# Expert weights from expert 11 on: gate and up in 22 KB pieces through three slot pairs, down tiles in single slots

## The chip, the core and the metric

The kernel runs on one core of a Trainium2 chip. The metric is device time in microseconds (us), the median of the runs. The weights lie in HBM and are brought into the core's own memory (SBUF) by DMA while TensorE (PE in the rows) multiplies. All weight transfers are issued from the queue of SyncE (SP, and SPq for its queue), one after the other in the order in which they stand there; an issue that waits holds up all that stand behind it.

## The reference: what is computed

One block of an encoder on 512 tokens of width 1024: a Fourier mixer and a state-space mixer, merged by gates, then a channel mixer of 16 experts, then a gated per-layer input and a last norm. The stage of this case is the mixer of experts:

```python
def expert_choice_ffn(h, w_router, w_gate, w_up, w_down):
    cap = EC_CAPACITY * s // N_EXPERTS            # 2 * 512 // 16 = 64 rows
    affinity = jax.nn.softmax((h @ w_router).astype(jnp.float32), axis=-1)
    vals, idx = lax.top_k(jnp.swapaxes(affinity, 1, 2), cap)
    xg = h[bidx, idx]
    hid = jax.nn.silu(jnp.einsum('becd,edf->becf', xg, w_gate)) * jnp.einsum('becd,edf->becf', xg, w_up)
    y = jnp.einsum('becf,efd->becd', hid, w_down) * vals[..., None].astype(h.dtype)
    ...
```

Each of the 16 experts takes 64 tokens and has three float32 matrices: gate and up of 1024 x 2816, down of 2816 x 1024. That is 11.5 MB each, 34.6 MB for an expert, and each byte is used once.

## The kernel before, in words

The experts run one after the other (L1867 on). An expert's part on TensorE is first `gate_up` (L1478): eight row blocks k of gate and up, 128 rows each, are multiplied with the 64 chosen tokens, whose transposed rows are the stationary operand. A piece of 128 x 2816 (one row block, 11 KB in each partition) feeds 6 matmuls in the source, which the trace counts as 12. Then the hidden rows are formed in three units of 512, 512 and 384 columns (`UNITS`, L957; ScalarE and VectorE, then a transpose on TensorE, L1508), and `down` (L1512) multiplies each unit with its tiles of the down matrix.

Weights come through a ring of ten slots of 11 KB, which lie two by two in five pairs (`big`, L952; tiles `wp` in the rows; pair 0 is named wp_2840, pair 1 wp_3047, pair 2 wp_2406, pair 3 wp_2528, pair 4 wp_2647). Beside them there are short slots of 8 KB, made from buffers that earlier work has left (`small`; tiles `w`). `weight_stream` (L977) lists all pieces in the order of use. `prefetch` (L1003) gives the next piece a slot by `take` (L1030) and records its DMA (L1017); if there is no slot the list waits. `done` (L1066), called where the matmuls of a piece end, gives its slot back and calls `prefetch(2)`. So the program fixes which piece follows which in a slot, and its DMA waits for the matmuls of the slot's former piece.

`paired(e)` (L965) is true for experts 0 to 5. Their gate and up rows come two row blocks at a time, 22 KB in each partition, into a whole pair, and their down tiles have three or four blocks (12 or 16 KB), also in a pair. From expert 6 on each piece takes one slot: gate and up come as 16 pieces of 11 KB, and down as 11 tiles of two blocks (8 KB). By then some slots hold things for good: `fin` (half of pair 0), `sel` (half of pair 1), and the four tiles `pg` of the per-layer gate matrix, of which three lie in short slots and the fourth in half of pair 4. `take` gives a down tile a short slot if one is free (`own`, which holds once `pg` 3 has its place), and otherwise a slot of the ring. From expert 11 on this leaves pairs 2 and 3 whole, one half each of pairs 0, 1 and 4, and three short slots.

The order on TensorE is written out by hand (`with ordered(E.PE)`): between the steps of `gate_up` and `down`, `spend` (L1826) puts in other work from two lists, by costs that each step yields: ranking, gathering and transposing for the next expert (L1461, L1662, L1421), and from expert 7 on the finish of rows that an expert has changed (L1705, L1729, L1742, L1748). The order on the other engines, SP's among them, is set by a scheduler, which places an instruction by what it waits for. GpSimd (POOL) issues the indirect fetches and stores of token rows.

Of the kernel before, what the change touches and what calls it, by code (L numbers as in the profile page):

```python
# [25 lines left out]
NE = 16  # L26
REDO = 9
SLACK = 0.9
START = 0
NSEL = 4  # L30
WX = 2.0
OPEN = 3
# [81 lines left out]
def block_kernel(ctx, tc, ins, cst, out, n_exp=NE, dbg=None, upto="end"):  # L114
# [837 lines left out]
    big, small = list(range(10)), []  # L952
# [12 lines left out]
    def paired(e):  # L965

        return e < NB - 1

    def down_tiles(e, u):

        q = UNITS[u][2]
        if paired(e):
            return [[(h, a) for a in range(q)] for h in range(2)]
        return [[(h, a), (h, a + 1)] for h in range(2) for a in range(0, q - 1, 2)] + (
            [[(h, 2) for h in range(2)]] if q == 3 else [])

    def weight_stream():  # L977
        for e in range(n_exp):
            if e == EMB:
                yield ("p", 0), None  # L980
                yield ("pp", 0), rows(ins["w_ple_proj"], 0)
                for i in range(2):
                    yield ("E", i), None
            if e == NB - 1:
                yield ("fin", 0, 0), None
                yield ("sel", 0, 0), None
            if e == NB:
                for i in range(4):
                    yield ("pg", i), rows(ins["w_ple_gate"], 2 * i)
            n = 2 if paired(e) else 1  # L990
            for k in range(0, 8, n):
                for w, nm in ((wg_, "g"), (wu_, "u")):
                    yield (e, nm, k), dap(w, (e * D + k // 2 * 2 * P + k % 2) * FE, [[2 * FE, P], [1, n * FE]])
            for u, (f0, _, q) in enumerate(UNITS):
                for i, blocks in enumerate(down_tiles(e, u)):
                    (h, a), (h1, _) = blocks[:2]
                    yield (e, "d", u, i), dap(wd_, (e * FE + h * HALF + f0 + a) * D,
                                              [[q * D, P], [HALF * D if h1 != h else D, len(blocks)], [1, D]])
# [21 lines left out]


    halves_left = {0: {0, 1}, 1: {2, 3}}
    pair_tiles = {}

    def slot_view(i, n=1):
        if i // 2 not in pair_tiles:
# [3 lines left out]
    def take(key):  # L1030


        rows_ = key[0] != "E" and len(key) == 3
        own = isinstance(key[0], str) and key[0] != "m" or ("pg", 3) in wt
        uid[0] += 1
        if not isinstance(key[0], str) and paired(key[0]):
            i = next((i for i in big if i % 2 == 0 and i + 1 in big), None)
            if i is None:
                return None
            big.remove(i)  # L1040
            big.remove(i + 1)
            home[key] = i, 2
            t = slot_view(i, 2)
            if not rows_:
                q = UNITS[key[2]][2]
                t = t[:, :q * D].rearrange("p (a n) -> p a n", a=q)
            wt[key] = t
        elif own and small and not rows_:
            pool, tag = home[key] = small.pop(0)
            t = pool([P, 2, D], f"w{uid[0]}", F32R if tag == "hl" else F32, tag=tag, bufs=2 if tag == "hl" else 1)  # L1050
            wt[key] = t[:].bitcast(F32) if tag == "hl" else t[:]
        else:
            alone = [i for i in big if i ^ 1 not in big]
            if not big:
                return None
            i = alone[0] if alone and own else big[0]
            big.remove(i)
            home[key] = i, 1
            t = slot_view(i)
            wt[key] = t if rows_ else t[:, :2 * D].rearrange("p (a n) -> p a n", a=2)  # L1060
        return wt[key]
# [100 lines left out]
    rows_, logs = {}, {}  # L1162
# [314 lines left out]

    def gate_up(e):  # L1478
        pgu = {nm: [xbank("g", 6) for _ in UNITS] for nm in "gu"}
        m = 2 if paired(e) else 1  # L1480
        for k, nm, j in [(k, nm, j) for k in range(0, 8, m) for nm in "gu" for j in range(m)]:
            w = get_w((e, nm, k))
            for pp, (f0, n, _) in zip(pgu[nm], UNITS):
                for h in range(2):
                    c0 = j * FE + h * HALF + f0
                    T.matmul(pp[64 * h:64 * h + 64, :n], XGT[e][:, (k + j) % 4, (k + j) // 4], w[:, c0:c0 + n],  # L1486
                             start=k + j == 0, stop=k + j == 7)
            if j == m - 1:
                done((e, nm, k))
            if k + j < 7 or nm == "g":  # L1490
                yield 1.0
        for u, (pg, pu, (_, n, _)) in enumerate(zip(pgu["g"], pgu["u"], UNITS)):
            t = ht
            S.activation(t[:, :n], pg[:, :n], AF.Tanh, scale=0.5)  # L1494
            V.scalar_tensor_tensor(t[:, :n], t[:, :n], 1.0, pg[:, :n], OP.add, OP.mult)  # L1495
            V.scalar_tensor_tensor(hids[u % 2][:, :n], t[:, :n], 0.5, pu[:, :n], OP.mult, OP.mult)  # L1496
            if u == 0:
                yield 1.0
            turn_hidden(e, u)
            yield 0  # L1500
# [432 lines left out]
```

## Time and profile before

| | us |
|---|---|
| median of 3 runs | 1737.38 |
| the three runs | 1737.38, 1733.82, 1737.91 |
| the profiled execution | 1737.61 |
| its span, first to last instruction | 1735.6 |
| around the span | 2.0 |

The span has three stretches: the mixers up to about 370 us, the experts up to about 1715 us, and 20 us of last rows. In the views a window is given in us from the start of the span; the DMA share is the mean busy share of the 16 DMA engines, and GB/s is what they moved. A row of the timeline has the start, the duration, the engine and line, the operation with its tiles, and in brackets how long the engine stood idle before it and who ended that. A row of a chain has a start, a duration and what took it; for a DMA the duration runs from its issue to its landing. Granted clock 1.00 is 2.4 GHz, 0.5 is 1.2 GHz. A row `PE ... <- DMA ...: a, n, b` says that PE waited a us in n waits for that transfer, the longest b.

### The profile page before, as it was taken

To read this page: it belongs to the slowest core of one execution; us is meant where nothing else is said; L and a number is where in the kernel's file an instruction comes from. 1 tells how busy PE (TensorE), PEld (TensorE's weight loads), DVE (VectorE), ACT (ScalarE), POOL (GpSimd) and SP (SyncE) were. 2 spreads that over 40 slices of the span, in tenths; PEclk is the share of its full clock that TensorE was granted. 3 is DMA by queue.
4 is the path that set the end of the run, shared out by engine and by line. 5 is a ranking of instruction groups with operands and counts; after the bars stand their busy time and mean duration, and the time that the engine had idled before them with its cause. 6 is when DMAs were issued, how large, how long until landed. Compare 5 with 4: busy or idle time off the path is not lost.

```text
span 1735.6 us, 19348 instructions
## 1 busy us (share of the span) xinstructions
PE 1584.8 (91%) x7982; PEld 746.5 (43%) x7982; DVE 509.1 (29%) x1063; ACT 350.2 (20%) x649; POOL 86.2 (5%) x134
## 2 busy tenths in 40 slices
PE   7998979999979998989886899999999998999896
PEld 6776768743323333323222344434344343433332
DVE  6898857332212021211111221212211112112011
ACT  4367443232101111010101010111111111111000
POOL 1000000110000000000000100000101000000000
PEclk9999989999999999999998999999999999999999
DMA  7622819589999999999999999999999999999994
GB/s 161 134 67 68 135 50 277 198 302 407 430 427 428 399 428 430 427 428 428 407 420 420 422 400 421 371 421 422 421 421 421 422 420 406 420 421 421 421 423 184
DMA packets 116440, 613.07 MB, mean 353 GB/s; under 512 B 25880, under 2 KB 59184, under 8 KB 72320
## 3 DMA queue, kind: packets, MB, share of 16 engines
q1 hardware_dynamic: 111648, 597.27, 87.3%
q0 software_dynamic: 4544, 14.49, 2.2%
q8 instruction: 63, 1.03, 0.3%
q14 instruction: 25, 0.20, 0.0%
q10 hardware_dynamic: 160, 0.07, 0.0%
HBM read 599.54 MB, written 12.78 MB: 353 GB/s over the span
## 4 chain that ended last, share of the span: by engine, by line
PE 42%; DMA 34%; ACT 1%; DVE 1%; issue 1%; SPq 0%; POOL 0%; POOLq 0%; ACTq 0%; DVEq 0%
PE px L1486 18%; DMA wp<-in_w_exp_gate_dram 14%; DMA wp<-in_w_exp_up_dram 13%; PE px L1521 12%; DMA wp<-in_w_exp_down_dram 5%; PE px L1748 3%; DMA w<-in_w_exp_down_dram 3%; PE px L1643 3%; PE px L1508 1%; PE px L1612 1%; PE px L1396 1%; PE px L1705 1%; ACT hT L1510 0%; PE px L1784 0%; PE px L1421 0%
## 5 line engine op out<-in xcount | busy, mean ns | idle before, releaser
L1486 PE MATMUL px<-wp,xgT 128*64 128x512 f32 (+1 forms) x3072 | 645.9, 566 | 65.8 <-DMA wp<-in_w_exp_gate_dram 47.7
L1486 PEld LDWEIGHTS px<-wp,xgT 128*64 128x64 f32 x3072 | 211.4, 138 | 473.1 <-issue 368.8
L1521 PE MATMUL px<-wp,hT 128*64 128x512 f32 x1200 | 281.4, 608 | 23.0 <-DMA wp<-in_w_exp_down_dram 15.8
L1521 PEld LDWEIGHTS px<-wp,hT 128*64 128x64 f32 x1200 | 81.0, 138 | 183.8 <-issue 142.8
L1242 DVE SCALAR_TENSOR_TENSOR junk<-xraw,aff,before 128x512 bf16<-128x512 f32 x60 | 44.9, 749 | 181.9 <-ACT xraw L1462 181.4
L1495 DVE SCALAR_TENSOR_TENSOR xraw<-xraw,px 128x512 f32<-128x512 f32 (+1 forms) x48 | 30.9, 643 | 129.0 <-ACT xraw L1494 128.8
L179 DVE TENSOR_TENSOR hl<-raw,hl 128x1024 fp32r<-128x1024 f32 (+1 forms) x45 | 53.8, 1198 | 38.4 <-ACT hl L178 38.4
L1537 DVE SCALAR_TENSOR_TENSOR xr<-px,aff,xr 128x512 f32<-128x512 f32 x56 | 40.0, 748 | 71.3 <-PE px L1536 71.3
L178 ACT CAST hl<-raw 128x1024 fp32r<-128x1024 f32 (+1 forms) x45 | 46.4, 1033 | 56.0 <-PE psm L184 24.8
L1494 ACT ACTIVATE xraw<-px 128x512 f32<-128x512 f32 (+1 forms) x48 | 27.0, 562 | 147.7 <-PE px L1486 86.4
L1521 PE MATMUL px<-w,hT 128*64 128x512 f32 x208 | 50.9, 619 | 5.2 <-ACT hT L1510 4.1
L1510 ACT COPY hT<-px 128x512 f32<-128x512 f32 (+1 forms) x48 | 26.4, 549 | 134.2 <-PE px L1508 133.5
L182 PE MATMUL psm<-xnH,hl 128*128 128x512 f32 x128 | 51.2, 400 | 0.1
L184 PE MATMUL psm<-xnH,hl 128*128 128x512 f32 x128 | 50.2, 392 | 0.7 <-DVE hl L179 0.5
L183 PE MATMUL psm<-xnL,hl 128*128 128x512 f32 x128 | 50.0, 390 | 0.0
L1901 DVE TENSOR_TENSOR xraw<-px,xraw 128x512 fp32r<-128x512 f32 x7 | 4.8, 692 | 147.3 <-ACT xraw L1900 147.3
L1643 PE MATMUL px<-w,wp 128*128 128x256 f32 x192 | 45.5, 387 | 0.0
L1748 PE MATMUL px<-w,xT 128*64 128x256 f32 x384 | 44.7, 382 | 0.0
L1508 PEld LDWEIGHTS px<-ident,xraw 128*128 128x128 f32 x176 | 24.8, 206 | 45.6 <-issue 30.2
L1462 ACT COPY xraw<-px 128x512 f32<-128x512 f32 x15 | 8.8, 585 | 174.4 <-PE px L1461 145.7
L1236 ACT ACTIVATE junk<-xraw,naff 128x512 bf16<-128x512 f32 x60 | 43.3, 722 | 1.9
L1508 PE MATMUL px<-ident,xraw 128*128 128x128 f32 x176 | 33.3, 308 | 11.0 <-DVE xraw L1496 9.6
(452 smaller groups left out, 1671.2 us busy)
## 6 DMA issues: line engine op xcount, KB each, us to landing
wp<-in_w_exp_gate_dram SPq DMA_DIRECT2D x80, 1408.0 KB
wp<-in_w_exp_up_dram SPq DMA_DIRECT2D x80, 1408.0 KB
wp<-in_w_exp_down_dram SPq DMA_DIRECT2D x84, 1024.0 KB
wp<-in_w_exp_gate_dram SPq DMA_DIRECT2D x24, 2816.0 KB
wp<-in_w_exp_up_dram SPq DMA_DIRECT2D x24, 2816.0 KB
wp<-in_w_exp_down_dram SPq DMA_DIRECT2D x24, 2048.0 KB
w<-in_w_exp_down_dram SPq DMA_DIRECT2D x26, 1024.0 KB
wp<-in_w_exp_down_dram SPq DMA_DIRECT2D x12, 1536.0 KB
```

What stands on the lines that cost most here:

```text
L178: S.copy(hi, src)
L179: V.tensor_tensor(lo, src, hi.bitcast(F32), OP.subtract)
L182: T.matmul(ps, lh, rh, start=first, stop=False)
L183: T.matmul(ps, lh, rl, start=False, stop=False)
L184: T.matmul(ps, ll, rh, start=False, stop=last)
L1236: S.activation(junk(n), rows[:, :n], AF.Sign, scale=2.0 ** 64, bias=naff[:, b, e:e + 1], accum_out=acc)
L1242: V.scalar_tensor_tensor(junk(n, "V"), rows[:, :n], aff[:, b, e:e + 1], before[:, b, cols], OP.is_equal, OP.mult, accum_out=acc)
L1486: T.matmul(pp[64 * h:64 * h + 64, :n], XGT[e][:, (k + j) % 4, (k + j) // 4], w[:, c0:c0 + n], start=k + j == 0, stop=k + j == 7)
L1508: T.transpose(ps[:, a * P:(a + 1) * P], hids[u % 2][:, a:q * P:q], ident)
L1521: T.matmul(PY[e][64 * dh:64 * dh + 64], hT[:, a, 64 * h:64 * h + 64], w[:, j, 512 * dh:512 * dh + 512], start=u == 0 and i == 0 and j == 0 ...
L1643: T.matmul(pg, xT[:, db], get_w(("pg", db // 2))[:, db % 2, cs], start=db == 0, stop=db == 7)
L1748: T.matmul(pg[64 * dh:64 * dh + 64], xT[:, db % 4, db // 4], get_w(("pg", db // 2))[:, db % 2, c1:c1 + 256], start=db == 0, stop=db == 7)
```

## The change

`LATE_PAIRS = 11` is new (an unused constant goes). `rows_paired(e)` is true for experts 0 to 5 as before and for 11 to 15. Where it is true, gate and up rows are listed as pieces of two row blocks (128 x 5632, 22 KB) and take a whole pair. `gate_up` then steps by two: gate k, gate k+1, up k, up k+1. `paired` still rules the down tiles, so those of experts 6 to 15 keep their form of two blocks (8 KB). In experts 11 to 15 (`keep`) a down tile takes a short slot, or else a ring slot whose partner is held for good; it may no longer break a free pair.

So that three pairs are whole, `sel` now takes a pair's half whose partner is free too, and that partner is set aside (`reserved`) for `pg` 3, which is listed later. `fin` shares pair 0 with one free half, `sel` and `pg` 3 fill pair 1, and pairs 2, 3 and 4 are whole.

```diff
--- before.py
+++ after.py
@@ -26,7 +26,7 @@
 NE = 16
 REDO = 9
 SLACK = 0.9
-START = 0
+LATE_PAIRS = 11
 NSEL = 4
 WX = 2.0
 OPEN = 3
@@ -966,6 +966,10 @@
 
         return e < NB - 1
 
+    def rows_paired(e):
+
+        return paired(e) or e >= LATE_PAIRS
+
     def down_tiles(e, u):
 
         q = UNITS[u][2]
@@ -987,7 +991,7 @@
             if e == NB:
                 for i in range(4):
                     yield ("pg", i), rows(ins["w_ple_gate"], 2 * i)
-            n = 2 if paired(e) else 1
+            n = 2 if rows_paired(e) else 1
             for k in range(0, 8, n):
                 for w, nm in ((wg_, "g"), (wu_, "u")):
                     yield (e, nm, k), dap(w, (e * D + k // 2 * 2 * P + k % 2) * FE, [[2 * FE, P], [1, n * FE]])
@@ -1020,7 +1024,7 @@
 
 
     halves_left = {0: {0, 1}, 1: {2, 3}}
-    pair_tiles = {}
+    pair_tiles, reserved = {}, {}
 
     def slot_view(i, n=1):
         if i // 2 not in pair_tiles:
@@ -1033,7 +1037,8 @@
         rows_ = key[0] != "E" and len(key) == 3
         own = isinstance(key[0], str) and key[0] != "m" or ("pg", 3) in wt
         uid[0] += 1
-        if not isinstance(key[0], str) and paired(key[0]):
+        weights = not isinstance(key[0], str)
+        if weights and (rows_paired(key[0]) if rows_ else paired(key[0])):
             i = next((i for i in big if i % 2 == 0 and i + 1 in big), None)
             if i is None:
                 return None
@@ -1051,10 +1056,18 @@
             wt[key] = t[:].bitcast(F32) if tag == "hl" else t[:]
         else:
             alone = [i for i in big if i ^ 1 not in big]
-            if not big:
+            keep = weights and rows_paired(key[0])
+            if key not in reserved and not (alone if keep else [i for i in big if i ^ 1 in big] if key[0] == "sel" else big):
                 return None
-            i = alone[0] if alone and own else big[0]
-            big.remove(i)
+            i = (alone[0] if alone and (own or keep) and key[0] != "sel" else
+                 next(i for i in big if key[0] != "sel" or i ^ 1 in big) if big else None)
+            if key in reserved:
+                i = reserved.pop(key)
+            else:
+                big.remove(i)
+            if key[0] == "sel":
+                big.remove(i ^ 1)
+                reserved[("pg", 3)] = i ^ 1
             home[key] = i, 1
             t = slot_view(i)
             wt[key] = t if rows_ else t[:, :2 * D].rearrange("p (a n) -> p a n", a=2)
@@ -1477,7 +1490,7 @@
 
     def gate_up(e):
         pgu = {nm: [xbank("g", 6) for _ in UNITS] for nm in "gu"}
-        m = 2 if paired(e) else 1
+        m = 2 if rows_paired(e) else 1
         for k, nm, j in [(k, nm, j) for k in range(0, 8, m) for nm in "gu" for j in range(m)]:
             w = get_w((e, nm, k))
             for pp, (f0, n, _) in zip(pgu[nm], UNITS):
```

The first place is SP's queue where expert 11 begins (`wp_...` are the slot pairs, and both 2816 halves of a pair bear its name). Before:

```order
L1017 DMA wp_3047<-in_w_exp_gate_dram 128x2816
L1017 DMA wp_2406<-in_w_exp_up_dram 128x2816
L1017 DMA wp_2406<-in_w_exp_gate_dram 128x2816
L1017 DMA wp_2528<-in_w_exp_up_dram 128x2816
L1017 DMA wp_2528<-in_w_exp_gate_dram 128x2816
L1017 DMA wp_2840<-in_w_exp_up_dram 128x2816
L1017 DMA wp_2647<-in_w_exp_gate_dram 128x2816
```

and now:

```order
L1021 DMA wp_2647<-in_w_exp_gate_dram 128x5632
L1021 DMA wp_2406<-in_w_exp_up_dram 128x5632
L1021 DMA wp_2528<-in_w_exp_gate_dram 128x5632
L1021 DMA wp_2647<-in_w_exp_up_dram 128x5632
L1021 DMA wp_2406<-in_w_exp_gate_dram 128x5632
```

Sixteen pieces an expert over seven slots in five pairs have become eight over three pairs.

The second place is the same queue at the end of expert 11 (`w_...` are short slots; the last gate or up row ahead of the tiles named down is expert 11's last piece, and gate or up rows after it are expert 12's). Before:

```order
L1017 DMA wp_2406<-in_w_exp_up_dram 128x2816
L1017 DMA w_6890<-in_w_exp_down_dram 128x2048
L1017 DMA w_6907<-in_w_exp_down_dram 128x2048
L1017 DMA w_6909<-in_w_exp_down_dram 128x2048
L1017 DMA wp_2406<-in_w_exp_down_dram 128x2048
L1017 DMA wp_2528<-in_w_exp_down_dram 128x2048 x2
L1017 DMA wp_2840<-in_w_exp_down_dram 128x2048
L1017 DMA wp_2647<-in_w_exp_down_dram 128x2048
L1017 DMA wp_3047<-in_w_exp_down_dram 128x2048
L1017 DMA wp_2406<-in_w_exp_down_dram 128x2048
L1017 DMA w_7056<-in_w_exp_down_dram 128x2x1024
L1017 DMA wp_2406<-in_w_exp_gate_dram 128x2816
```

and now:

```order
L1021 DMA wp_2406<-in_w_exp_up_dram 128x5632
L1021 DMA w_6897<-in_w_exp_down_dram 128x2048
L1021 DMA w_6940<-in_w_exp_down_dram 128x2048
L1021 DMA w_6942<-in_w_exp_down_dram 128x2048
L1021 DMA wp_2840<-in_w_exp_down_dram 128x2048
L1021 DMA wp_2528<-in_w_exp_gate_dram 128x5632
L1021 DMA w_7042<-in_w_exp_down_dram 128x2048
L1021 DMA w_7058<-in_w_exp_down_dram 128x2048
L1021 DMA w_7064<-in_w_exp_down_dram 128x2048
L1021 DMA wp_2840<-in_w_exp_down_dram 128x2048
L1021 DMA w_7075<-in_w_exp_down_dram 128x2048
L1021 DMA wp_2647<-in_w_exp_up_dram 128x5632
```

Three of eleven down tiles had short slots, and the others took ring slots that gate and up pieces had left. Now four tiles have slots when the last piece is issued; each of the other seven stands behind the matmuls of an earlier down tile of the same expert, and the scheduler has put a gate piece of the next expert behind the fourth. It did the same at the ends of experts 12 and 13; there two and one of the four tiles stand ahead of the expert's last piece.

The third place is the same queue at the end of expert 14. It is drawn from the changed program; in the one before it looks as at the end of expert 11.

```order
L1021 DMA wp_2406<-in_w_exp_up_dram 128x5632
L1021 DMA w_8083<-in_w_exp_down_dram 128x2048
L1021 DMA w_8126<-in_w_exp_down_dram 128x2048
L1021 DMA w_8128<-in_w_exp_down_dram 128x2048
L1021 DMA wp_2840<-in_w_exp_down_dram 128x2048
L1021 DMA w_8179<-in_w_exp_down_dram 128x2048
L1021 DMA w_8195<-in_w_exp_down_dram 128x2048
L1021 DMA w_8201<-in_w_exp_down_dram 128x2048
L1021 DMA wp_2840<-in_w_exp_down_dram 128x2048
L1021 DMA w_8212<-in_w_exp_down_dram 128x2048
L1021 DMA w_8227<-in_w_exp_down_dram 128x2048
L1021 DMA w_8233<-in_w_exp_down_dram 128x2x1024
```

Here no piece of expert 15 stands between the fourth and the fifth down tile, nor is there any at the end of expert 15, the last.

## Rows read from the trace of the kernel before

**Rows 1.** The profile's page: 40 slices, DMA busy share in tenths and GB/s.

```profile
DMA  7622819589999999999999999999999999999994
GB/s 161 134 67 68 135 50 277 198 302 407 430 427 428 399 428 430 427 428 428 407 420 420 422 400 421 371 421 422 421 421 421 422 420 406 420 421 421 421 423 184
```

**Rows 2.** The page's DMA issues: tile, queue, count, KB each.

```profile
wp<-in_w_exp_gate_dram SPq DMA_DIRECT2D x80, 1408.0 KB
wp<-in_w_exp_down_dram SPq DMA_DIRECT2D x84, 1024.0 KB
wp<-in_w_exp_gate_dram SPq DMA_DIRECT2D x24, 2816.0 KB
```

**Rows 3.** Windows of gate and up transfers: window, length, PE busy, clock, DMA share, GB/s.

```profile
672.00:722.00 50.00, 45.69 (x212) 0.97 1.00 429
753.00:803.00 50.00, 44.45 (x202) 0.97 1.00 427
...
1288.00:1336.00 48.00, 48.00 (x272) 1.00 1.01 422
1373.00:1423.00 50.00, 50.00 (x280) 1.00 1.01 422
1459.00:1509.00 50.00, 49.17 (x280) 1.00 1.01 418
1545.00:1595.00 50.00, 45.95 (x258) 1.00 1.01 422
1630.00:1680.00 50.00, 46.68 (x264) 1.00 1.01 423
```

**Rows 4.** The same columns over whole experts: 3 to 5, and 11 to 15.

```profile
600.00:850.00 250.00, 229.05 (x1049) 0.98 1.01 425
...
1285.00:1712.00 427.00, 399.27 (x2135) 0.99 1.01 418
```

**Rows 5.** PE's longest waits for DMA from 1285 to 1371, then from 1543 to 1628.

```profile
PE px L1486 <- DMA wp<-in_w_exp_up_dram: 0.2, 1, 0.2
...
PE px L1521 <- DMA wp<-in_w_exp_down_dram: 3.0, 5, 0.9
```

**Rows 6.** The chain that ended last: two pieces, from issue to landing.

```profile
1321.79 22.19 DMA wp<-in_w_exp_up_dram
...
1567.03 19.06 DMA wp<-in_w_exp_up_dram
```

**Rows 7.** Timeline of PE: last piece and first down tile, experts 11 to 15.

```profile
1344.02 2.58 PE L1486 MATMUL px<-wp,xgT 128*64 128x512 f32 x12 [0.21 <-DMA wp<-in_w_exp_up_dram]
1351.87 1.94 PE L1521 MATMUL px<-w,hT 128*64 128x512 f32 x8 [0.68 <-ACT hT L1510]
...
1431.28 2.58 PE L1486 MATMUL px<-wp,xgT 128*64 128x512 f32 x12
1436.93 1.94 PE L1521 MATMUL px<-w,hT 128*64 128x512 f32 x8 [0.68 <-ACT hT L1510]
...
1520.57 2.58 PE L1486 MATMUL px<-wp,xgT 128*64 128x512 f32 x12
...
1600.63 2.58 PE L1486 MATMUL px<-wp,xgT 128*64 128x512 f32 x12 [0.81 <-DMA wp<-in_w_exp_up_dram]
1604.56 1.94 PE L1521 MATMUL px<-w,hT 128*64 128x512 f32 x8 [0.68 <-ACT hT L1510]
...
1685.49 2.58 PE L1486 MATMUL px<-wp,xgT 128*64 128x512 f32 x12 [1.42 <-DMA wp<-in_w_exp_up_dram]
1689.43 1.94 PE L1521 MATMUL px<-w,hT 128*64 128x512 f32 x8 [0.68 <-ACT hT L1510]
```

**Rows 8.** Timeline of PE: the last of the eleven down tiles of expert 15.

```profile
1712.93 1.94 PE L1521 MATMUL px<-w,hT 128*64 128x512 f32 x8 [0.58 <-DMA w<-in_w_exp_down_dram]
```

**Rows 9.** Timeline at the start: a 4 KB transfer and its reader.

```profile
1.14 0.65 ACTq L282 DMA_DIRECT2D g<-in_g_mix_dram  x1
...
3.76 0.24 PE L320 MATMUL pss<-ident,g 8*128 8x8 f32 x1 [3.76 <-DMA g<-in_g_mix_dram]
```

## The prediction

> **What bounds the kernel now.** I read the page's slices first. From the tenth slice on the 16 DMA engines are full and move about 420 GB/s to the end of the experts [rows 1]; at 1.01 of the time they leave nothing idle in the stretch of experts 11 to 15 [rows 3, 4]. Bytes set the time there, and nothing that only rearranges waits on TensorE can shorten it. The second view is the windows of gate and up transfers. Where the pieces are 2816 KB they run at 429 and 427 GB/s, where they are 1408 KB at 422, 422, 418, 422 and 423 [rows 2, 3]: 428.0 against 421.4 on the mean. That is the whole of what the change can win in rate. The third view is the timeline of PE at the last piece of each expert. Those of experts 11 to 15 start at 1344.02, 1431.28, 1520.57, 1600.63 and 1685.49 [rows 7], so 87.3, 89.3, 80.1 and 84.9 us apart. In the last of these periods PE waits for weights; in expert 11 it waits 0.2 us for them [rows 5], and in two windows it is busy for 48.00 of 48 and 50.00 of 50 us [rows 3]. So TensorE is slower than the transfers in experts 12 and 13, and the transfers stay full only because much is asked for ahead: a piece lands 22.19 or 19.06 us after its issue [rows 6], though its own transfer takes 1.4418 MB / 421.4 GB/s = 3.4 us. Both sides are near their limit, and what joins them is the stock of free slots. The change deals with just that.
>
> **Gate and up in 22 KB pieces: the gain.** Experts 11 to 15 have 5 x 16 of the 160 pieces of 1408 KB (80 gate and as many up, [rows 2]), 115.3 MB. At 421.4 GB/s they take 273.7 us, at 428.0 they take 269.5: **4.2 us less**, all of it on the path as long as the engines stay full. That only 40 DMAs are issued in place of 80 costs or brings nothing by itself, since SP waits for slots and not for its own issuing.
>
> The Trainium skill ("DMA: Bandwidth & Descriptors", Rules for kernel authors) asks for transfers of 1 MiB or more for full bandwidth and sets nothing above that. Both sizes are over it, so by this rule the gain is nothing and the sum below comes to +6.1; the windows show 421.4 and 428.0, and I follow them, with the rule as a rival.
>
> **What 22 KB costs on TensorE.** A piece is usable only when all of it has landed. The last piece of an expert is now 24 matmuls and not 12, so what follows its landing starts later by one block of 12, 2.58 us in the rows, or 2.4 us from start to start. I take 2.4. Within an expert this costs nothing while PE is behind the transfers anyway, as in experts 11 to 13; in 14 and 15 PE has waits to give up [rows 5].
>
> **Down tiles that wait for finished blocks.** Before, a down tile takes slots that gate and up pieces have left, long before PE comes to it. Now four tiles have slots, and each of the other seven waits at SP until a down block of the same expert is done; everything behind it in SP's queue waits with it. The question is whether the DMA engines run dry meanwhile. From the start of the last piece to the end of the first down block it takes 9.8, 7.6, 5.9, 5.9 and 5.9 us in experts 11 to 15 [rows 7] (for expert 13, whose down row is not shown, I take the 5.9 of the two after it). With the 2.4 us from above that is 12.2, 10.0, 8.3, 8.3 and 8.3. A DMA issued then has some 2.6 us until it acts, by the small transfer at the start, issued at 1.14 and used at 3.76 [rows 9]. So the fifth tile's data cannot come before 14.8, 12.6, 10.9, 10.9 and 10.9 us after the last piece.
>
> What fills this time? A down tile takes (1712.93 - 1685.49) / 11 = 2.5 us at the end of the kernel [rows 7, 8], a 22 KB piece 2.884 MB / 428 GB/s = 6.7 us. Behind the last piece stand, by the order of SP's queue, four tiles and a gate piece in expert 11 (16.7 us), two tiles and a gate piece in 12 (11.7), three and a gate piece in 13 (14.2), and four tiles in 14 and 15 (10.0). The shortfalls are 0, 0.9, 0, 0.9 and 0.9: **2.7 us**. After that a tile per 1.9 us of PE asks for the next 2.5 us of transfer, so the queue fills again. If the gate pieces did not go ahead, the shortfalls would be 4.8, 7.6, 3.4, 0.9 and 0.9, 17.6 us. So 2.7 and 17.6 are the ends; I take the lower, since a gate piece needs only the pair of the last piece but two, whose matmuls are over by then.
>
> A second sentence of the Trainium skill speaks against issuing late: one DMA pays about 2.0 us besides bytes / 436 GB/s ("DMA: Bandwidth & Descriptors", Anatomy of one DMA, written for issues from GpSimd). By it the three shortfalls would be 0.3 each and the sum lower by 1.8; the row of 4 KB, 2.62 us, lies close to it and is the one I use.
>
> **The thinner stock.** While PE works on one pair, two pairs can be on their way, 13.4 us of transfer, where 22 us lay between issue and landing. PE falls behind by 87.3 - 84.9 = 2.4 us in expert 12 and by 89.3 - 84.9 = 4.4 in 13, 6.8 together [rows 7], and wins 4.8 back in 14. Before, the stock took this up. Now a late `done` may find the queue empty. No row shows the engines with so thin a stock, so the bounds are 0 (the 13.4 us suffice) and 6.8 (none of the lateness is taken up); a gain from thinness has no mechanism. I take the middle, **3.4 us**: 13.4 is about two thirds of what there was, and the first three hand-overs use it too. A dip of the clock is in that price: the 0.97 in two rows of paired experts [rows 3] is 1.2 GHz for 3 us of 50, 1.5 us of TensorE work.
>
> **The rest.** `sel` sets a slot aside for `pg` 3 one expert early. Expert 6 then has six slots where it had seven; that is 3.4 us of stock out of some twenty, hidden by the full queue of a stage in which PE waits for bytes, and at most 3.4 us if it were not. Fetches of token rows share the engines with larger pieces and may land later; they are issued tens of us before their use, so I cost them at nothing. PE's order changes from g, u, g, u to g, g, u, u with the same matmuls, which moves other work by a step: nothing.
>
> **The sum.** -4.2 + 2.7 + 3.4 = +1.9 us against the profiled execution of 1737.61, which is 0.2 above the median: 1739.3, said as 1739. Ends of the same terms: -4.2 with both losses at 0 gives 1733; the shortfalls as taken and all the lateness, -4.2 + 2.7 + 6.8 = +5.3, gives 1743.
>
> **The rivals.**
> - *The hand-overs run dry (slower).* The gate piece between the fourth and the fifth tile is itself late, because its pair is still held by a piece that PE has not reached, and SP, which goes in order, holds the tiles behind it. Then 17.6 takes the place of 2.7: -4.2 + 17.6 = +13.4, 1751, with the lateness counted in it. It decides from the point at which PE is more than 6.7 us behind the transfers at an expert's end. For it: PE's full windows and the 89.3 us period [rows 3, 7]. Against it: the experts with the longest PE are only two.
> - *The larger piece brings no rate.* The difference of the windows is that of other traffic in the stages, and not of piece size. Then 0 + 2.7 + 3.4 = +6.1, 1743.5. Against it: the five windows of small pieces lie within 418 to 423, and the two of large ones at 427 and 429.
> - *The stage runs like experts 3 to 5 (faster).* The windows over whole experts show 425 and 418 GB/s [rows 4]. 427 us at 418 is 178.5 MB; at 425 it takes 420.0 us, 7.0 less: 1730.4. Against it: a third of the bytes, the down tiles, keep their 1024 KB.
>
> **How the numbers follow.** A measurement of this kernel tells 0.3%, 5.2 us, from no change. The forecast (1733 to 1743, all but its edge within 0.3%) has 0.65, the dry hand-overs 0.20, no gain in rate 0.09, the fast stage 0.06. The dry hand-overs may be partial, which puts some of their chance between 1743 and 1751. Faster by over 0.3% has the fast stage's 0.06; slower has 0.20 and most of the 0.09, 0.27; within 0.3% is left with 0.67. For 8 in 10 I leave out the fast stage and the upper part of the dry hand-overs: 1733 to 1747.
>
> **What would show it.** In the changed profile the gate and up windows of experts 11 to 15 should read 427 to 429 GB/s, with the DMA share at 1.00 but for short dips below it behind the last piece of experts 12, 14 and 15. If the share falls for 5 us or more at the ends of 11 to 13, the dry hand-overs are right; if the windows stay at 421 with a full share, the rate is the wrong step. PE's waits for down tiles (5 waits of at most 0.9 us in expert 14 [rows 5]) should grow. The last down tile should start within 6 us of 1712.93 [rows 8]; the tail behind it, 22.7 us to the span's end, stays. The forecast is wrong if pieces are used at another pace than the last-piece times say, above all if the thin stock idles the engines inside the gate and up stretches, which I price only through PE's lateness.

## The result, and the profile after

The changed kernel takes **1751.08 us** (median of 6 runs, 1748.82 to 1755.03), the kernel before beside it 1733.60 (1732.63 to 1737.91). The ratio is 1.0099, with a 95% interval from 1.0081 to 1.0117: 17 us slower, outside the forecast range. The profiled execution of the changed kernel is the fastest of its runs (1748.82, span 1747.0), and that of before was at the upper end of its own; so the two traces are 11.4 us of span apart, not the 17.5 of the medians, and the sums below are made against those 11.4. Where the other 6 us lie no trace shows.

The page's slices, DMA busy share in tenths and GB/s, answer to [rows 1]:

```profile
DMA  7722829589999999999999999999999998999994
GB/s 160 133 73 72 128 58 319 161 339 409 429 426 429 400 427 430 425 432 418 412 418 422 417 400 413 382 421 422 420 418 428 397 423 349 408 426 409 412 403 171
```

Before, every slice from the 27th to the 39th read 420 to 423 but one. Now they go up and down between 349 and 428. The windows of the changed kernel (window, length, PE busy and matmuls, clock, DMA share, GB/s) show it closer, and answer to [rows 3, 4]:

```profile
1281.00:1329.00 48.00, 45.35 (x256) 1.00 1.01 429
1440.00:1450.00 10.00, 6.16 (x46) 1.00 0.88 338
1450.00:1460.00 10.00, 9.95 (x39) 0.83 0.87 323
1480.00:1490.00 10.00, 9.71 (x44) 1.00 0.79 293
1508.00:1535.00 27.00, 25.43 (x142) 1.00 1.01 422
1560.00:1608.00 48.00, 45.69 (x262) 1.00 1.00 418
1646.00:1690.00 44.00, 42.76 (x246) 1.00 1.00 419
1281.00:1724.00 443.00, 402.29 (x2137) 0.99 0.98 404
```

The last row is the whole stage of experts 11 to 15: 443 us at a share of 0.98 where it was 427 at 1.01. Three rows show the largest dips: the end of expert 12 (1440 to 1460) and the first pieces of expert 13 (1480 to 1490). PE's waits for weights in that stage (line, what it waits for: total, times, longest), where [rows 5] had 5 waits of at most 0.9 us for down tiles in expert 14:

```profile
PE px L1534 <- DMA w<-in_w_exp_down_dram: 13.9, 15, 2.5
PE px L1499 <- DMA wp<-in_w_exp_gate_dram: 6.5, 2, 4.9
PE px L1499 <- DMA wp<-in_w_exp_up_dram: 5.9, 6, 1.5
```

The chain that ended last now goes through down tiles too, from issue to landing (start, length); the gate and up pieces of [rows 6] had 19 and 22 us of lead:

```profile
1353.64 6.53 DMA w<-in_w_exp_down_dram
...
1374.49 9.11 DMA w<-in_w_exp_down_dram
```

A tile that is asked for this late has no lead at all: PE stands ready for it. The last down tile of the kernel starts at 1724.27 instead of 1712.93 [rows 8]; the 22.7 us behind it are unchanged.

```profile
1724.27 1.94 PE L1534 MATMUL px<-w,hT 128*64 128x512 f32 x8 [0.55 <-DMA w<-in_w_exp_down_dram]
```

### The profile page after: what moved, and what is told of

The parts are those of the page before. It is cut to its first block, busy times and chain, and to the rows that moved or that the text cites. A ratio compares the mean times of both kernels' runs of the same rounds, so it can differ in the third digit from the quotient of the medians.

```text
span 1747.0 us, 19250 instructions
## 1 busy us (share of the span) xinstructions
PE 1587.2 (91%) x7982; PEld 747.5 (43%) x7982; DVE 509.5 (29%) x1063; ACT 350.5 (20%) x649; POOL 87.6 (5%) x134
## 4 chain that ended last, share of the span: by engine, by line
PE 42%; DMA 34%; ACT 1%; DVE 1%; issue 1%; POOL 0%; POOLq 0%; SPq 0%; ACTq 0%; DVEq 0%
PE px L1499 18%; DMA wp<-in_w_exp_gate_dram 14%; DMA wp<-in_w_exp_up_dram 13%; PE px L1534 13%; DMA w<-in_w_exp_down_dram 4%; DMA wp<-in_w_exp_down_dram 3%; PE px L1656 2%; PE px L1761 2%; PE px L1521 1%; PE px L1625 1%; PE px L1718 1%; PE px L1409 1%; ACT hT L1523 0%; PE px L1797 0%; PE px L1474 0%
## 5 line engine op out<-in xcount | busy, mean ns | idle before, releaser
L1534 PE MATMUL px<-wp,hT 128*64 128x512 f32 x1000 | 235.0, 608 | 18.8 <-DMA wp<-in_w_exp_down_dram 11.6
L1534 PEld LDWEIGHTS px<-wp,hT 128*64 128x64 f32 x1000 | 67.6, 138 | 152.5 <-issue 119.1
L1534 PE MATMUL px<-w,hT 128*64 128x512 f32 x408 | 100.2, 620 | 18.6 <-DMA w<-in_w_exp_down_dram 14.4
L1534 PEld LDWEIGHTS px<-w,hT 128*64 128x64 f32 x408 | 27.0, 140 | 72.3 <-issue 46.2
L1764 DVE SCALAR_TENSOR_TENSOR esel<-xraw,esel 128x256 f32<-128x256 f32 x16 | 6.8, 425 | 125.6 <-ACT xraw L1763 125.6
## 6 DMA issues: line engine op xcount, KB each, us to landing
wp<-in_w_exp_gate_dram SPq DMA_DIRECT2D x44, 2816.0 KB, 17.5
```

What stands on the lines that cost most here:

```text
L1534: T.matmul(PY[e][64 * dh:64 * dh + 64], hT[:, a, 64 * h:64 * h + 64], w[:, j, 512 * dh:512 * dh + 512], start=u == 0 and i == 0 and j == 0 ...
```

## The experiments

The theories have letters in the expectations. A: the rule for down tiles costs. B: the 22 KB pieces in pairs cost. C: the place of `sel` and `pg` 3. D: PE has no time to spare, so that each of its waits is passed on to the transfers. E: the amount of stock alone. F: free slots which the next piece in the order may not take. Each kernel was timed beside the kernel before on the same chip.

### The change taken apart

Down tiles may break a pair again, pieces stay 22 KB (`e_break`):

```
-if key not in reserved and not (alone if keep else ... else big):
+if key not in reserved and not (... else big):
```

> The changed kernel with one thing undone: from expert 11 on gate and up rows still come as 22 KB pieces, but a down tile that finds no short slot left over may again take one half of a free pair. Theory A (the loss comes from the down tiles, which wait for short slots and then stand behind 22 KB pieces in the queue): the waits of PE for down tiles of experts 11 to 14 go, 13.9 us in the changed kernel back to about 1, and the time is 1730 to 1738 us. Theory B (three pairs of 22 KB pieces are too thin a stock, whatever the down tiles do): the waits for gate and up stay or grow, and the time is 1746 to 1754 us.

Measured 1752.90, ratio 1.0101 (1.0081 to 1.0121). The waits for down tiles went as A said, and the time did not:

```profile
PE px L1499 <- DMA wp<-in_w_exp_gate_dram: 13.8, 5, 4.9
PE px L1499 <- DMA wp<-in_w_exp_up_dram: 9.5, 8, 2.1
...
PE px L1534 <- DMA w<-in_w_exp_down_dram: 1.9, 4, 0.5
```

13.9 us of waits for short slots became 1.9, and 12.4 us for gate and up became 23.3. The waits name what comes late, not why. In this kernel the engines stand still ahead of expert 12's first gate piece. It is issued at 1371.07, after the down matmuls whose end frees a slot; the down tiles had broken the pairs, so no whole one was there earlier. The window, and SP's wait there (what it waits for: total, times, longest):

```profile
1361.00:1371.00 10.00, 7.10 (x49) 0.92 0.52 213
```

```profile
SPq L1021 <- PE px L1534: 13.8, 1, 13.8
```

The opposite half, 11 KB pieces with the slots divided as in the changed kernel (`e_keep11`):

```
-return paired(e) or e >= LATE_PAIRS
+return paired(e)
+free = [i for i in big if (i >= 4) == rows_] if ... key[0] >= LATE_PAIRS else big
```

> The kernel before's 11 KB pieces for experts 11 to 15, with the changed kernel's division of the slots alone: gate and up pieces only into the three pairs from slot 4 on, down tiles only into the four slots below. Theory A (the division of the slots costs): down tiles are late as in the changed kernel, 1743 to 1752 us. Theory B (the size of the pieces costs): 1732 to 1738 us, as before the change.

Measured 1752.02, ratio 1.0092 (1.0071 to 1.0113): all of the loss again, as A said, without one 22 KB piece in these experts. So A and B are each right in half: either restriction alone costs what both cost together. Here the engines stand still before the down tiles that wait for finished down blocks, at the ends of experts 11 and 12. The windows, and SP's wait in the second:

```profile
1350.00:1355.00 5.00, 4.23 (x24) 1.00 0.46 182
1451.00:1461.00 10.00, 8.62 (x28) 0.66 0.49 180
```

```profile
SPq L1021 <- PE px L1535: 10.7, 1, 10.7
```

In both kernels SP waits for down matmuls of the expert that is ending (L1534, L1535), for the sake of another piece each time.

SP in the written order (`e_strict`):

```
-    with ordered(E.PE):
+    with ordered(E.PE, E.SP):
```

> The changed kernel with SP issuing its transfers strictly in the written order, so that no gate or up piece of the next expert goes ahead of a down tile that waits for its slot. Theory A1 (the down tiles are late because 22 KB pieces of the next expert were put ahead of them): 1740 to 1746 us, waits for down tiles under 6 us. Theory A2 (the down tiles are late because their slots come free late, and the pieces ahead only fill the queue meanwhile): the DMA queue runs dry while SP waits, and the time is 1756 to 1766 us, slower than the changed kernel.

Measured 1773.61, ratio 1.0217 (1.0199 to 1.0234). A2 is right in kind, and its range was 8 us too low: the pieces that go ahead fill the queue, and without them it costs 22 us more than the change. The stage takes 462 us at a share of 0.94:

```profile
1289.00:1751.00 462.00, 407.46 (x2135) 0.97 0.94 387
```

The place of `sel` and `pg` 3 alone (`e_sel`, `LATE_PAIRS = 16`):

> The changed kernel's code with the border for 22 KB pieces set past the last expert: what is left of the change is the place of the selection tile and of the last piece of the per-layer gate, which now take a free pair. All theories but C: 1731 to 1736 us, no difference from before. Theory C (that placement costs): 1740 us or more.

Measured 1735.18, ratio 1.0005 (0.9992 to 1.0017). C falls.

### How much stock

A piece only where another slot stays free, two in `b_hold2` (`b_hold1` is shown), in the kernel before:

```
-            if not big:
+            if len(big) <= (1 if not isinstance(key[0], str) and key[0] >= 11 else 0):
```

> The kernel before, with one change: from expert 11 on a weight piece is issued only if one further 11 KB slot would stay free, so that one slot of the ten (1.44 MB) always stands empty. Pieces, order and choice of slots stay as they were. Theory E (the stage's time goes by how much is queued for the DMA engines: they run dry in short gaps whenever free slots stand unfilled, whatever leaves them so): the queue is shorter by 1.4 MB and the time 1738 to 1746 us. Theories A and B (the place of down tiles, the size of pieces): neither is changed, 1733 to 1737 us.

> The same with two slots of the ten (2.9 MB) always left empty. Theory E: 1748 to 1762 us, so that two empty slots cost at least what the change costs. Theories A and B: 1733 to 1738 us.

Measured 1735.33 (1.0000, 0.9989 to 1.0012) and 1739.63 (1.0025, 1.0013 to 1.0037). The first says nothing: what is issued and not yet used is 10.0 MB on the mean in its trace as in that of before, since the DMA waits for the matmuls that last read its slot and not for the place where it is recorded. The second did leave pair 3 nearly out, two of seven ring slots: its halves take 6 pieces in the program where they took 32 (7.8 MB). So I took slots away by name (`b_minus1`: half of pair 4, slot 8; `b_minus3`, shown: that and pair 2):

```
+            out_ = (4, 5, 8) if not isinstance(key[0], str) and key[0] >= 11 else ()
+            free = [i for i in big if i not in out_]
```

> The kernel before with one of the seven ring slots (half of the last pair) not used from expert 11 on, pieces and choice otherwise free. Theory E (the loss follows the amount of stock alone): +2 to +4 us, 1737 to 1740 us. Theory F: under +3, 1733 to 1738 us.

> The same with three of the seven ring slots not used (a pair and that half), which leaves less stock than the changed kernel has. Theory E: 1748 us or more, the changed kernel's loss at its amount of stock. Theory F: 1739 to 1747 us, less than the changed kernel although it has more slots, since here every free slot is filled at once.

Measured 1735.27 (0.9996, 0.9986 to 1.0005) and 1748.84 (1.0064, 1.0047 to 1.0081). One slot of seven is worth nothing, two are worth 0.25%, three 0.64%. E cannot explain the changed kernel by the mean: it has 8.4 MB issued and unused, more than the kernel with five slots, and loses four times as much.

Whole pairs for the down tiles too (`a_pair` from expert 11, `a_pair7` from expert 7):

```
-        return e < NB - 1
+        return e < NB - 1 or e >= LATE_PAIRS
```

> The changed kernel with the down weights of experts 11 to 15 also in whole slot pairs (tiles of four or three row blocks, 16 and 12 KB, as in the first experts), so that no slot is kept for one kind and any free pair takes the next piece. Theory E: nothing stands empty by its kind, the loss of 17 us is mostly gone and the gain of the longer pieces is seen: 1729 to 1741 us. Theory B (pieces of 22 KB in pairs are too coarse whatever else is done): 1746 us or more.

> The same from expert 7 on, so that nearly all weights come in whole pairs; in experts 7 to 10 PE sets the pace and DMA has time over. Theory E: within 5 us of the version from expert 11 on, 1728 to 1744 us. Theory B: the same loss again for the further experts or at least 1750 us.

Measured 1763.00 (1.0163, 1.0137 to 1.0189) and 1776.41 (1.0242, 1.0214 to 1.0270). My expectation was wrong. Nothing is kept for a kind here, but tiles of 12 and 16 KB cannot use the short slots at all, which I had overlooked: 6.8 MB are issued and unused on the mean, and the engines are idle for 24 us. The experiment changes more than it was to, and does not tell E from F.

### PE's spare time, and how many experts

Both kernels with six of eight row blocks of the recomputed gate left out (`light_before`, `light_after`):

```
-            for db in range(8):
+            for db in (range(8) if e < 10 else (0, 7)):
```

> The kernel before with less work for PE: in the recomputed gate of experts 10 to 15, six of the eight row blocks of the gate's matmuls are left out (96 matmuls of 64x256 each expert, some 5.4 us of PE), all transfers stay. By every theory the stage stays bound by the transfers: 1726 to 1735 us.

> The changed kernel with the same work left out. Theory D (the change is dear because PE has almost no time over in experts 11 and 12, so that each wait for a down tile delays the slots of the next expert): with 5.4 us more of spare PE time per expert the change costs at most 5 us over the kernel before with the same work left out. Theory F (the queue runs dry at each hand-over because free slots may not take what is next in the order, whatever PE has to spare): it costs 10 to 17 us as before.

Measured 1733.47 (0.9995, 0.9981 to 1.0008) and 1746.50 (1.0066, 1.0046 to 1.0087). The first shows that the stage was bound by transfers alone: over 20 us less PE work, and no gain. The second costs 13.0 us over the first, where the change cost 17.5; F's range was met and D's was not, so D is a small part at most. The stage of both, first before, then here:

```profile
1284.00:1711.00 427.00, 378.33 (x1895) 1.00 1.01 419
```

```profile
1283.00:1722.00 439.00, 380.63 (x1897) 0.98 0.98 408
```

The border at expert 13 (`e_13`) and at 15 (`e_last`), by `LATE_PAIRS`:

> The changed kernel with the border at expert 13 instead of 11, so that two of the four hand-overs inside the stage are left, those of experts 13 and 14. Theory D (the waits hurt in experts 11 and 12, where PE set the pace before): 1735 to 1741 us. Theory F (a like price for each hand-over): half of the loss or more, 1742 to 1747 us.

> The changed kernel with the border at expert 15: only the last expert's gate and up rows come as 22 KB pieces, no expert follows whose pieces could be late, and its down tiles still take short slots alone. By both theories within 4 us of the kernel before, 1732 to 1739 us; over 1743 would say that the last hand-over alone costs much.

Measured 1751.82 (1.0096, 1.0076 to 1.0116) and 1739.11 (1.0022, 1.0009 to 1.0035). With the border at 15 little is left, as expected. With the border at 13 two hand-overs fewer saved nothing, but this is no test of D or of a price per hand-over, because the trace shows one standstill that the changed kernel does not have, where the pairs begin:

```profile
1452.00:1462.00 10.00, 10.00 (x65) 1.00 0.25 99
```

SP issues the first gate piece of expert 13 only at 1461.04, after a wait of 13.5 us for down matmuls whose end makes a pair whole. PE is busy in all of the window and meets the gap later. This standstill is 7.7 us of the 14.7 us in which the engines are idle in that stage.

### Order, release, transfer

The kernel before with the changed order (`b_order`), and with both pieces of a kind given back together (`b_coarse`):

```
+        for k, nm, j in ([(k + i, nm, 0) for k in range(0, 8, 2) for nm in "gu" for i in range(2)] if late else
+            if late and k % 2:
+                done((e, nm, k - 1))
+                done((e, nm, k))
```

> The kernel before with the changed order of gate and up from expert 11 on (gate k, gate k+1, up k, up k+1, in the transfers and on PE), each piece still 11 KB in any free slot, given back after its own 12 matmuls. If the order costs: over 1740 us. By theory F (free slots that the next piece may not take) nothing changes: 1733 to 1737 us.

> The same, but the two pieces of a kind are given back together after 24 matmuls, as a 22 KB piece is, while each next piece may still take any free slot. If the coarse release costs: 1743 us or more. By theory F: 1733 to 1740 us, since a released slot is refilled at once, and one slot of the stock more or less was worth 0.4 us.

Measured 1735.67 (1.0005, 0.9996 to 1.0015) and 1734.45 (0.9998, 0.9988 to 1.0008). The order costs nothing. The second says nothing, for the same reason as `b_hold1`: its stock is that of before, so slots were still refilled after 12 matmuls.

The changed kernel's slots with two transfers of 11 KB for each piece (`e_two`):

```
+                for j in range(2):
+                    Q.dma_start(t[:, j * FE:(j + 1) * FE], ap[j])
```

> The changed kernel with each 22 KB piece issued as two transfers of 11 KB into the two halves of its slot pair; slots, order and releases are those of the changed kernel. If the long transfer itself costs (PE may not begin on half of it): 1736 to 1746 us. By theory F the slots decide and the two halves bring 3 us at most, while the rate falls back to that of 11 KB pieces, +4: 1749 to 1756 us.

Measured 1753.05, ratio 1.0112 (1.0095 to 1.0129), 1 us from `e_keep11` and 2 from the changed kernel, within the intervals. With the slots so divided, the length of the transfers neither costs nor brings anything that can be seen, and pairs on top of the division cost nothing more.

Two 11 KB pieces with interleaved matmuls in the kernel before (`b_inter`):

```
+                    for j in range(2):
+                        T.matmul(pp[64 * h:64 * h + 64, :n], XGT[e][...], ws[j][:, c0:c0 + n], ...)
```

> The kernel before with the matmuls of two 11 KB pieces interleaved from expert 11 on (each output tile takes a matmul of the one and then of the other), so that PE begins only when both have landed and both slots come free within two matmuls of each other, as with a 22 KB piece; the pieces still take any free slot. If coarse landing and release cost: 1743 us or more. By theory F (the loss comes from free slots that the next piece may not take): 1733 to 1740 us.

Measured 1747.85, ratio 1.0068 (1.0051 to 1.0085). It looks like a verdict for coarse release and is none, because the interleaving made PE itself slower. PE's busy time in the gate and up matmuls from 1290 to 1690, first before, then here:

```profile
1290.00:1690.00 400.00, 197.28 (x960) 0.99 1.01 419
```

```profile
1290.00:1690.00 400.00, 209.03 (x918) 0.99 0.99 409
```

197.28 / 960 is 0.206 us of busy time for each matmul, 209.03 / 918 is 0.228. Over the stage PE is busy 417.64 us of 439, where it was 399.27 of 427 [rows 4].

```profile
1284.00:1723.00 439.00, 417.64 (x2143) 0.99 0.99 407
```

### What they say together

From each trace I worked out four things for the stage, from the first packet of expert 11's gate and up to the end of the last weight packet: its length; the time of all DMA packets (summed and divided by 16 engines; packets on one engine overlap a little, so this can exceed the length); the idle time of the engines, summed over steps of 0.25 us in which their share is under 0.95; and the weights that are issued and whose matmuls are not done (the stock, up to the last issue).

| kernel | time against before | length | packets | idle | stock mean, lowest (MB) |
|---|---|---|---|---|---|
| before | | 427.7 | 431.3 | 1.2 | 10.0, 7.3 |
| `b_order` | 1.0005 | 427.2 | 431.2 | 0.7 | 10.0, 7.3 |
| `b_minus1` | 0.9996 | 427.5 | 431.9 | 0.3 | 9.1, 7.2 |
| `light_before` | 0.9995 | 426.6 | 430.8 | 0.6 | 9.8, 7.3 |
| `b_hold2` | 1.0025 | 431.7 | 434.6 | 1.6 | 7.8, 5.6 |
| `e_last` | 1.0022 | 431.1 | 432.4 | 3.0 | 9.4, 3.1 |
| `b_inter` | 1.0068 | 436.7 | 433.6 | 7.8 | 9.6, 7.3 |
| `b_minus3` | 1.0064 | 443.0 | 437.1 | 10.3 | 6.4, 4.3 |
| changed | 1.0099 | 441.2 | 434.9 | 9.2 | 8.4, 3.1 |
| `light_after` | 1.0075 (to `light_before`) | 437.5 | 430.3 | 10.3 | 8.5, 3.1 |
| `e_keep11` | 1.0092 | 444.1 | 436.0 | 12.5 | 7.5, 3.1 |
| `e_two` | 1.0112 | 445.1 | 436.2 | 13.1 | 7.5, 3.1 |
| `e_13` | 1.0096 | 446.2 | 435.1 | 14.7 | 8.4, 3.1 |
| `e_break` | 1.0101 | 444.1 | 431.5 | 15.8 | 8.2, 5.0 |
| `a_pair` | 1.0163 | 453.2 | 431.1 | 24.0 | 6.8, 3.1 |
| `e_strict` | 1.0217 | 460.7 | 436.1 | 27.4 | 7.3, 3.1 |

The packets take 430 to 437 us in every kernel, so most of what moves the length is idle time. The mean stock does not order the kernels. The lowest does somewhat better: those that keep over 7 MB lose nothing (but for `b_inter`, whose matmuls are slower), and those that come down to 3.1 MB lose 0.75% or more. Two fall out. `e_last` comes down to 3.1 MB in the last expert alone and loses 0.22%; `e_break` never falls under 5.0 MB and loses 1%: what had landed there was of no use to the next piece, which found no pair. What is shown: the transfers of this stage have no time to spare, and the change makes the engines stand still in short stretches and move some packets slowly, whichever of the two restrictions is kept. What stays open: whether in `e_break` it is the matching of two halves or the release after 24 matmuls, since neither `b_coarse` nor `b_inter` tried the second alone.

## Why the prediction was wrong

**The bound was right.** Transfers set the time; `light_before` shows it directly. Order of use and the place of `sel`, priced at nothing, are nothing (`b_order`, `e_sel`). The tail is the same.

**The gain in rate, -4.2, is the step that failed.** The prediction has it "all of it on the path as long as the engines stay full", and they did not stay full. With the idle time left out, the engines needed 432.0 us for the stage (441.2 less 9.2) where they had needed 426.5: +5.5, not -4.2. That is 9.7 of the 11.6 us by which this trace misses the forecast of +1.9. By the size of the packets (time of all of them, divided by 16 engines):

| packets | before | changed |
|---|---|---|
| gate and up, 11 KB (10240), then 22 KB (5120) | 274.8 | 273.4 |
| down tiles, 8 KB (6407, 6405) | 126.0 | 131.6 |
| 4 KB | 27.8 | 27.8 |

The typical gate and up packet does bring the gain: its median is 836 ns where two of 11 KB took 2 x 426 = 852, which is 5.1 us over 5120 packets and 16 engines, and expert 11's first window has the 429 GB/s that the term wanted. But some packets are far slower. 269 of the 22 KB packets and 386 of the 8 KB packets took over 1.05 of their median (10 of 8 KB before), and what slow packets of all sizes took beyond their medians adds up to 12.7 us where it was 1.8. Of it, 10.9 us lie where less than 4 MB of weights were issued and not yet moved; the changed kernel spends 64% of its weight packets' time in that state, the one before 17%. So the later full windows read 422, 418 and 419, as [rows 3] had for 1408 KB, and the down tiles, which keep their form and had no term, lost 5.6 us. I carried a rate over from a stage with a full queue. Why a packet is slow with so little behind it is not settled. Nor is the size of the term the same in each trace: from `light_before` to `light_after` the time without idle goes from 426.0 to 427.2, +1.2. A gain of 4.2 is in neither pair. By the Trainium skill ("DMA: Bandwidth & Descriptors", Rules for kernel authors) both sizes have full bandwidth; over the stage no gain was measured, as by that rule, though the first window and the medians show that a difference exists.

**The hand-overs, +2.7, were right up to the fifth tile and too low behind it.** From the start of the last piece to the issue of the fifth tile it took 13.9, 11.3, 9.0, 8.3 and 8.3 us in experts 11 to 15, where I had 12.2, 10.0, 8.3, 8.3 and 8.3; in the first three PE puts other work between the two halves of the last piece. The engines were idle ahead of the fifth tile's data for 0.4, 1.3, 0, 0.9 and 0.6 us, 3.1 in sum, where I had 0, 0.9, 0, 0.9 and 0.9. What failed is the sentence behind it, "so the queue fills again": behind the fifth tile there are 2.2 us more of idle time in small gaps, 1.6 of them in expert 12, where I had none. PE's timeline there:

```profile
1440.93 1.94 PE L1534 MATMUL px<-w,hT 128*64 128x512 f32 x8 [0.68 <-ACT hT L1523]
...
1443.11 2.81 PE L1761 MATMUL px<-w,xT 128*64 128x256 f32 x24
1445.76 1.03 PE L1761 MATMUL px<-wp,xT 128*64 128x256 f32 x8
1449.95 0.74 PE L1521 MATMUL px<-ident,xraw 128*128 128x128 f32 x4 [3.17 <-DVE xraw L1509]
1450.63 5.35 PE L1534 MATMUL px<-w,hT 128*64 128x512 f32 x16
```

SP's queue, with the fourth piece of expert 13 at the end:

```profile
1442.91 0.33 SPq L1021 DMA_DIRECT2D w<-in_w_exp_down_dram  x1
1443.28 0.47 SPq L1021 DMA_DIRECT2D wp<-in_w_exp_up_dram  x1
1453.64 2.71 SPq L1021 DMA_DIRECT2D w<-in_w_exp_down_dram  x2
...
1468.48 0.46 SPq L1021 DMA_DIRECT2D wp<-in_w_exp_gate_dram  x1
1472.31 0.33 SPq L1021 DMA_DIRECT2D w<-in_w_exp_down_dram  x1
1484.62 0.33 SPq L1021 DMA_DIRECT2D wp<-in_w_exp_up_dram  x1
```

and the windows around these issues (a packet counts where it starts):

```profile
1442.00:1445.00 3.00, 3.00 (x26) 1.00 0.61 162
1445.00:1453.00 8.00, 4.83 (x30) 0.90 1.01 424
1453.00:1457.00 4.00, 4.00 (x16) 0.78 0.78 241
1482.00:1487.00 5.00, 5.00 (x27) 1.00 0.57 168
```

The dip of the first window is the forecast one, ahead of the fifth tile, which is issued at 1442.91. Then the second down block begins 9.7 us after the first, since PE has the recomputed gate and a wait for DVE between them, and SP issues nothing from 1443.28 to 1453.64. That looks like the loss and is little of it: one tile and one 22 KB piece, 2.5 + 6.7 us of transfer, keep the engines full until 1453, and they are idle for 0.8 us behind it. The kernel before, which the prediction reads as without any idle time in this stage, has the same stretch, and is idle for 1.0 us around its end:

```profile
1438.90 0.38 SPq L1017 DMA_DIRECT2D w<-in_w_exp_down_dram  x1
1453.73 0.33 SPq L1017 DMA_DIRECT2D wp<-in_w_exp_gate_dram  x1
```

With most of the recomputed gate left out (`light_after`) the idle time of the stage is 10.3 us, not less.

**The thinner stock, +3.4, came out at 3.6, by its mechanism and with luck in the number.** The engines are idle for 3.6 us inside gate and up, 2.4 us of it in the last window above. The third pair is filled at 1468.48, and the fourth piece waits 12.0 us for the first 24 matmuls of expert 13, which PE begins at 1476.19. From 1468.48 to 1484.62 there are 9.2 us of transfer for 16.1 us. This is the late `done` that the prediction names; but 3.4 was the middle of two bounds, and PE's lateness does not measure it, since `light_after` has 3.3 us at the same place.

**The sum.** The idle time of 9.2 us is 3.1 and 2.2 in the hand-overs, 3.6 in gate and up and 0.3 at the ends of the stage. It grew by 8.0 (from 1.2) where I had 2.7 + 3.4 = 6.1, and the time without idle by 5.5 where I had -4.2: 13.5 us instead of 1.9. Expert 11's first packet came 2.1 us earlier in this execution (1280.1 for 1282.2), which leaves the 11.4 us of span.

**The rivals.** The dry hand-overs gave 1751, which is the measured time, but not by the way described: the hand-overs are idle for 5.3 us and not 17.6, SP is not held by a late gate piece, and PE's lateness at an expert's end is not what decides, since 13.0 of 17.5 us stay with a lighter PE. `e_strict` shows that the pieces ahead do cover, by 22 us rather than the 14.9 between 17.6 and 2.7. "No gain in rate" was right in its outcome but not in its reason, since the larger packet is faster while the queue is full. The two could come at once, 17.6 against the 17.5 between the medians, and I had treated them as exclusive; but with the hand-overs working in another way than described, that the numbers meet is chance.

## What to carry to other kernels

Where transfers set the time, list for a change of buffers the stretches in which SP can issue nothing: for each the two issues around it, what is queued at the first, and all that PE does until it frees the slot for the second. Then read the share of the engines in just that stretch: here 10 us without an issue cost 0.8 us. A rate that was read with a full queue holds only while the queue is full; price the thin queue separately, for the pieces that do not change too. A rule that says which piece may use which free slot, by kind or by whole pairs, cost 1% here, where one slot less for all pieces cost nothing and two 0.25%. And a wait that disappears from PE's list is no gain as long as the engines' idle time stays: in `e_break` 12 us of waits changed their name only.

## What was not expected of the hardware

Interleaving two pieces, so that two matmuls in a row write the same 64 of the 128 output rows (`b_inter`), cost 0.228 us of busy time for each gate and up matmul, against 0.206 where they alternate, but not evenly. 48 in a row kept the old pace of 0.20 us, and 12 behind other work took 0.27:

```profile
1302.70 9.67 PE L1487 MATMUL px<-wp,xgT 128*64 128x512 f32 x48
...
1323.85 3.22 PE L1487 MATMUL px<-wp,xgT 128*64 128x512 f32 x12
```

The stationary tile also changes from one matmul to the next there, and no run tells the causes apart.

With little in the queue some DMA packets take far longer while the median does not rise (8 KB: mean 315 to 329 ns, median 313 to 309), and most of what they lose lies where under 4 MB are issued and not yet moved (10.9 of 12.7 us). No run here tells why.
